# Both token tiles evacuated before their transposes, eleven low parts moved to VectorE, and a fourth bank for small products, in a two-block hybrid layer

## The chip, the cores and the metric

The kernel runs on one core of one Trainium2 chip, as one program of 39576 instructions. The metric is the device time of a run in microseconds; the median of three runs of the kernel before is 2757.88 us. Below, PE is the matrix engine (TensorE), DVE is VectorE, ACT is ScalarE, POOL is GpSimd and SP is the engine that issues most transfers.

## What is computed

The input `x` has 256 tokens of 2048 values. It goes through two blocks, each a mixer and a feed-forward network around residual additions, with shift, scale and gate vectors ("modulation") computed from a conditioning vector:

```
h = rmsnorm(x) * (1 + sc_m) + sh_m ;  x = x + gt_m * rmsnorm(mixer1(h) @ w_out)
h = rmsnorm(x) * (1 + sc_f) + sh_f ;  x = x + gt_f * rmsnorm(relu(h @ w_ff1)**2 @ w_ff2)
u = rmsnorm(x) * (1 + sc1) + sh1   ;  x = x + g1 * (mixer2(u) @ w_out_2)
u = rmsnorm(x) * (1 + sc2) + sh2   ;  x = x + g2 * ((silu(u @ w_gate) * (u @ w_up)) @ w_down)
return rmsnorm(x)
```

`mixer1` holds two linear-attention forms (8 heads each), `mixer2` four attention forms (named fox, nsa, dil and diff in the code). All is float32; the modulation is a vector of 2048 values times a matrix of 2048 x 12288, once for each block.

## The kernel before, in words

**Weights and blocks.** A weight matrix is read in units of 128 x 1024 values (512 KB) into one of five `raw` buffers. ScalarE copies a unit to a rounded high part `wh`; VectorE or GpSimd subtracts it from the unit and writes the low part `wl`; then `raw` is free for the next transfer. High and low parts lie in four or six slots. PE multiplies high by high, high by low and low by high, and adds the three up in PSUM. A `Block` is one slice of output columns (512, or 256 in most of the feed-forward blocks); it takes its units one after the other and its result stays in two of the four PSUM banks named `g`. The units of the modulation are not converted: VectorE multiplies each by a column of the conditioning vector and adds it into `acc` (their transfers and updates stand between those of the weights, in one list, `items`). In the kernel's first part the modulation goes through PE instead, into a PSUM bank of its own (`ps["a"]`, line 2007).

**Small products.** Transposes, attention scores and the like take a bank by `mx()` (line 210) from a ring of three PSUM banks. Who asks for a bank gets that of the third call before, and waits until that product has been read. `run_last` (581) also takes one block's two result banks from this ring (`mbanks`, 503).

**Order of the work.** The order of instructions on each engine is written out by the program itself, with a model of the engines' clocks (`_Clock`). While PE runs a block, `fill` (453) is called after each k-tile (after every second one in blocks of 256 columns, which makes eight calls a block). Each call advances the first generator of the queue `pri` by one step, then one urgent filler, then up to two fillers and up to two weight preparations (`prep`, 285), as the model finds them due. A generator's `yield` ends its step. `run` (567) first empties `pri` down to one generator. Engines work strictly in the order written; an instruction that waits holds back all that stand behind it on its engine.

**The opening blocks.** The first block of each feed-forward network runs on the raw float32 weights, before the others are converted (`run_first`, 607): `("f1",0,0)` with `ev_relu2_s` (1430), `("ga",0,0)` with `ev_gate2_s` (1903). Its results lie with tokens as rows, one bank for each of the two token tiles, and must be transposed. Both functions go through the tiles one after the other: evacuate the tile (ScalarE and VectorE), pause for seven steps, take a bank, four transposes on PE, evacuate again. So the second tile is evacuated after the first one's transposes.

**Where low parts go.** `LOW` (1955 to 1957) gives blocks of the second mixer the value 3; for their units `l_eng` (364) chooses GpSimd or VectorE by the model's clocks, GpSimd unless it would end over 3 us later. Units without a value go to VectorE. `qG` and `kvH` are the first two converted blocks of that mixer, eight units each. `late_prep` (373) reckons with the same choice.

Of the kernel before, what the change touches and what calls it, by code (L numbers as in the profile page):

```python
# [9 lines left out]
F32 = mybir.dt.float32  # L10
# [168 lines left out]
def two_blocks(ctx, tc, I, out):  # L179
    nc = tc.nc  # L180
    PSUM = bass.MemoryType.PSUM
# [12 lines left out]
    def opener(name, side, **kw):  # L194
        cm = tc.tile_pool(name=name, side=side, **kw)
        return cm.__enter__(), partial(cm.__exit__, None, None, None)
# [11 lines left out]
    ps = {}  # L208

    def mx():  # L210
        return ps["m"].tile([128, 512], F32, name="mx", tag="mx")

    def wt(name="wt"):
        return w2.tile([128, 512], F32, name=name, tag="wt")
# [206 lines left out]
    def pri_step():  # L421
        q = pri.popleft()
        try:
            next(q)
        except StopIteration:
            return
        pri.appendleft(q)

    def fill_step(force=False, fillers=fillers):
        k = None  # L430
        for i, (at, q) in enumerate(fillers):
            if force or at <= clk.t["pe"] + lag[0]:
                key = at - lead.get(q, 0.0)
                if k is None or key < best:
                    k, best = i, key
        if k is None:
            return False
        at, q = fillers.pop(k)
        clk.end = 0.0
        try:  # L440
            next(q)
        except StopIteration:
            return True
        fillers.append((clk.end if clk.end else max(at, clk.t["pe"]) + 0.3, q))
        return True
# [3 lines left out]
    def add(q, before=0.0):  # L449
        lead[q] = before  # L450
        fillers.append((clk.t["pe"], q))
# [15 lines left out]
    def drain(until=lambda: False):  # L467
        while (pri or fillers or urgent) and not until():
            if pri:
                pri_step()  # L470
            fill_step(True, urgent)
            fill_step(True)


    def units(w, r0, nkt, c0, n):
        u = []
        for k in range(0, nkt, UK):
            ap = w[r0 + k * 128:r0 + (k + UK) * 128, c0:c0 + n].rearrange("(k p) f -> p k f", p=128)
            u.append(([(0, 128, 0, UK, 0, ap)], UK, n))
        return u  # L480
# [22 lines left out]
    def mbanks():  # L503
        return [mx(), mx()]

    def banks():
        return [psg.tile([128, 512], F32, name="g", tag="g") for _ in range(2)]
# [31 lines left out]
    def run_units(b, pts, idx, pos):  # L539
        for i in idx:  # L540
            prep_to(i + 1)
            it = items[i]
            for kk in range(it["nk"]):
                if b.kind == "S":
                    mm_s(b, pts, it, kk, pos, (0, 1))
                else:
                    mm_t(b, pts, it, kk, pos)
                pos += 1
                if kk == it["nk"] - 1:
                    used(i)  # L550
                if b.n != 256 or kk % 2:
                    fill()
        return pos
# [9 lines left out]
    def add_acc(b, pts, out):  # L563
        for p, a, o in zip(pts, b.acc, out):
            dve.tensor_tensor(o, p, a, op=ADD)

    def run(b):
        while len(pri) > 1:
            clk.end = 0.0
            pri_step()  # L570
            if not clk.end:
                fill_step(True)
        pts = b.pts or banks()
        run_units(b, pts, b.idx, len(b.kts) - sum(items[i]["nk"] for i in b.idx))
        if b.acc:
            add_acc(b, pts, b.acc)
            add(b.done(b.acc))
        elif b.done:
            pri.append(b.done(pts))
# [90 lines left out]
    r = rows[3]  # L670
# [27 lines left out]
    def first_cols():  # L698
        rslots.extend((RAW_BUFS + k, pro) for k in range(3))
        dma_to(len(items))  # L700
        p = mx()
        pe.transpose(p[:, 0:32], rows[3][0:32], ident[0:32, 0:32])
        act.activation(cols[:, 0:32], p[:, 0:32], AF.Copy)
        th = small([32], "th32")
        act.activation(th, p[:, 0:32], AF.Tanh, scale=0.5)
        dve.scalar_tensor_tensor(csil, th, 1.0, cols[:, 0:32], op0=ADD, op1=MUL)
        dve.tensor_scalar(csil, csil, 0.5, None, op0=MUL)

    def more_cols():
        p = mx()  # L710
        for i in range(3):
            pe.transpose(p[:, i * 128:(i + 1) * 128], rows[i], ident)
        act.activation(cols[:, 32:384], p[:, 32:384], AF.Copy)
# [101 lines left out]
    def new_hT(quads=range(4)):  # L815
        if 0 in quads:
            hT["n"] = [0, 0]
        for q in quads:
            t = hT["b", q] = hTp.tile([128, 4, 2, T], FR, name=f"hT{q}", tag=f"hT{q}")
            hT["h", q], hT["l", q] = t[:, :, 0], t[:, :, 1]  # L820
# [90 lines left out]
    def plan(key, b):  # L911
        blocks[key] = b
        order.append(key)
# [496 lines left out]
    def new_r(q):  # L1410
        p = oTp if q < 3 else g["rp"]
        rT[q] = tuple(p.tile([128, 4, T], FR, name=f"r{a}{q}", tag=f"o{a}{q}") for a in "hl")
# [16 lines left out]

    def ev_relu2_s(pts):  # L1430
        new_r(0)
        for t in range(2):
            r = wt("relu")
            act.activation(r, pts[t], AF.Relu)
            dve.scalar_tensor_tensor(r, pts[t], 0.0, r, op0=MAX, op1=MUL)
            for _ in range(7):
                yield
            p = mx()
            for j in range(4):
                pe.transpose(p[:, j * 128:(j + 1) * 128], r[:, j * 128:(j + 1) * 128], ident)  # L1440
            h, l = (x[:, :, t * 128:(t + 1) * 128] for x in rT[0])
            p4 = p.rearrange("p (a b) -> p a b", a=4)
            act.activation(h, p4, AF.Copy)
            dve.tensor_sub(l, p4, h)

    plan(("f1", 0, 0), Block("S", units(w_ff1, 0, KT, 0, 512), list(range(16)), hsrc, ev_relu2_s))
    for ch in range(4):
        for q in range(4):
# [452 lines left out]
        return ev  # L1901

    def ev_gate2_s(pts):
        for t in range(2):
            th = wt("th")
            act.activation(th, pts[t], AF.Tanh, scale=0.5)
            dve.scalar_tensor_tensor(th, th, 1.0, pts[t], op0=ADD, op1=MUL)
            for _ in range(7):
                yield
            p = mx()  # L1910
            for j in range(4):
                pe.transpose(p[:, j * 128:(j + 1) * 128], th[:, j * 128:(j + 1) * 128], ident)
            act.activation(g["sg2"][:, 0, :, t * 128:(t + 1) * 128], p.rearrange("p (a b) -> p a b", a=4), AF.Copy)
            yield

    plan(("ga", 0, 0), Block("S", units(w_g, 0, KT, 0, 512), KS, hsrc, ev_gate2_s))
    for ch, nq in ((0, 4), (1, 4), (2, 3)):
        for q in range(nq):
# [35 lines left out]

    LOW = {k: 1 for k in ("qG", "kvH", "sv", "qA", "kB", "qC", "kD", "dv0", "dv1", "qE", "kF", "fdv")}
    LOW.update({k: 3 for k in LOW if isinstance(k, str)})
    LOW.update({("pA", c): 2 for c in range(4)})
    ai = n_first
    wide = [blocks[n, 0] for n in ("hq", "hf", "hv", "hg", "zq", "zk", "zv", "gg")]
# [49 lines left out]
    x = pro.tile([128, 2, D], F32, name="x")  # L2009
# [155 lines left out]
    g["x"] = xp.tile([128, 2, D], F32, name="xres")  # L2165
    act.dma_start(g["x"], I["x"][0].rearrange("(t p) d -> p t d", p=128))
    drain(lambda: gwn.get("gt_m") == 4)
    run(blocks["oB", 0])
    new_hT(range(3))
    close_more = more_slots("hl2")  # L2170
# [104 lines left out]
    t = hTp.tile([128, 4, 2, T], FR, name="oq2", tag="hT3")  # L2275
# [66 lines left out]
    x = g["x"]  # L2342
# [75 lines left out]
```

## Time and profile before

| what | us |
|---|---|
| median of three runs | 2757.88 |
| lowest and highest run | 2756.11, 2759.71 |
| the profiled execution, its own time | 2756.43 |
| its span, first to last instruction | 2754.7 |
| PE busy in the span | 2629.3 |
| VectorE, ScalarE, GpSimd busy | 1814.2, 1260.8, 410.0 |
| granted clock of PE, mean | 0.981 |

The stages in the span: modulation and first mixer up to about 740 us, first feed-forward network to about 1480, second mixer to about 1990, second feed-forward network to the end. In the timelines a row gives start, length, engine, operation, its output and inputs by name, how many of them, and in brackets how long the engine stood idle before it and what released it. All instructions have line L169, the helper that records them, so they are told apart by names: `mx` is a small product, `g` a block's result, `relu` and `th` what the two functions evacuate, `S` attention scores.

### The profile page before, as it was taken

What the parts mean: (1) busy time and instruction counts of PE and PEld (TensorE: products, weight loads), DVE (VectorE), ACT (ScalarE), POOL (GpSimd) and SP (SyncE); (2) the same over time, 40 slices, a digit from 0 to 9 for tenths busy, and PEclk for the clock granted to TensorE, in tenths of its full rate; (3) what the DMA queues carried; (4) which work ended last, traced back from release to release, by engine and by line L of the source; (5) the groups of instructions that cost most, each with busy time, mean ns of one, the idle gap of its engine ahead of it and who ended that gap; (6) DMA issues with size and microseconds to landing.
All of it is one profiled execution on the core that took longest, in us unless ns stands there. A gap on an engine that the chain in (4) does not pass through costs nothing.

```text
span 2754.7 us, 39576 instructions
## 1 busy us (share of the span) xinstructions
PE 2629.3 (95%) x15073; PEld 2207.5 (80%) x15073; DVE 1814.2 (66%) x2247; ACT 1260.8 (46%) x2124; POOL 410.0 (15%) x262
## 2 busy tenths in 40 slices
PE   7999889899999999999999899898889999999998
PEld 4788879868678888888886888886668888888887
DVE  3557878854667787878854365558756756554566
ACT  2434443444544454444544355544444444443443
POOL 1001242231000000000001555562400000000001
PEclk9999999999999999999999999998999999999999
DMA  9975878985488989989964765666667777666664
GB/s 354 322 255 153 229 201 219 275 253 174 156 267 275 322 286 306 320 279 331 300 191 155 232 186 184 213 225 223 203 207 243 233 247 224 193 194 192 189 187 145
DMA packets 399806, 643.59 MB, mean 234 GB/s; under 512 B 31480, under 2 KB 198088, under 8 KB 398208
## 3 DMA queue, kind: packets, MB, share of 16 engines
q1 hardware_dynamic: 391904, 627.03, 71.7%
q10 hardware_dynamic: 6960, 11.65, 1.2%
q8 instruction: 118, 1.93, 0.3%
q0 software_dynamic: 752, 2.39, 0.2%
q14 instruction: 72, 0.59, 0.1%
HBM read 636.27 MB, written 4.19 MB: 233 GB/s over the span
## 4 chain that ended last, share of the span: by engine, by line
PE 59%; DMA 4%; DVE 4%; POOL 2%; issue 2%; ACT 2%; SPq 0%; POOLq 0%; ACTq 0%; DVEq 0%
PE g L169 56%; PE mx L169 3%; POOL wl L169 1%; DMA raw<-in_w_in_dram 1%; DMA raw<-in_w_out_dram 1%; DVE wl L169 1%; DMA raw<-in_w_ff_dram 1%; ACT wh L169 1%; DVE acc L169 1%; DVE y L169 1%; DVE xres L169 0%; DMA raw<-in_ffn_w_up_dram 0%; DMA raw<-in_ada_w_dram 0%; DMA raw<-in_ffn_w_gate_dram 0%; DVE S L169 0%
## 5 line engine op out<-in xcount | busy, mean ns | idle before, releaser
L169 ACT ACTIVATE wh<-raw 128x1024 fp32r<-128x1024 f32 (+2 forms) x793 | 823.8, 1045 | 896.7 <-PE g L169 406.0
L169 PE MATMUL g<-hT,wh 128*128 128x512 f32 (+1 forms) x4448 | 1218.0, 345 | 9.1 <-ACT wh L169 4.8
L169 DVE TENSOR_TENSOR wl<-raw,wh 128x1024 fp32r<-128x1024 f32 x693 | 858.0, 1245 | 549.8 <-ACT wh L169 545.5
L169 PE MATMUL g<-hT,wl 128*128 128x256 f32 x3376 | 954.9, 283 | 10.3 <-DVE wl L169 5.5
L169 PEld LDWEIGHTS g<-hT,wh 128*128 128x128 f32 x4448 | 772.9, 191 | 125.8 <-issue 18.9
L169 PEld LDWEIGHTS g<-hT,wl 128*128 128x128 f32 x3376 | 644.4, 191 | 14.0 <-DVE wl L169 6.9
L169 DVE SCALAR_TENSOR_TENSOR acc<-raw,csil,acc 128x1024 f32<-128x1024 f32 x276 | 382.3, 1385 | 59.8 <-DMA raw<-in_ada_w_dram 58.6
L169 PE MATMUL g<-wh,rh 128*128 128x512 f32 x864 | 339.0, 392 | 0.0
L169 PE MATMUL g<-wh,rl 128*128 128x512 f32 x864 | 338.9, 392 | 0.0
L169 PE MATMUL g<-wl,rh 128*128 128x512 f32 x864 | 338.6, 392 | 0.0
L169 POOL TENSOR_TENSOR wl<-raw,wh 128x1024 fp32r<-128x1024 f32 (+2 forms) x100 | 230.1, 2311 | 222.7 <-ACT wh L169 211.2
L169 PEld LDWEIGHTS g<-wh,rl 128*128 128x128 f32 x864 | 162.3, 188 | 36.0
L169 PEld LDWEIGHTS g<-wl,rh 128*128 128x128 f32 x864 | 162.4, 188 | 35.7
L169 PEld LDWEIGHTS g<-wh,rh 128*128 128x128 f32 x864 | 162.3, 188 | 35.8
L169 PE MATMUL g<-wh,hT 128*128 128x512 f32 (+2 forms) x544 | 162.9, 371 | 1.8 <-ACT hq L169 1.8
L169 PEld LDWEIGHTS g<-wh,hT 128*128 128x128 f32 x544 | 98.5, 191 | 28.1 <-issue 13.0
L169 POOL TENSOR_TENSOR y<-yy,gw 128x512 f32<-128x512 f32 x6 | 7.7, 1298 | 704.3 <-DVE yy L169 704.3
L169 PE MATMUL g<-wl,hT 128*128 128x512 f32 (+2 forms) x272 | 98.8, 363 | 4.1 <-DVE wl L169 2.0
L169 POOL TENSOR_TENSOR y<-y,gw 128x512 f32<-128x512 f32 x6 | 9.6, 1625 | 558.6 <-DVE y L169 553.2
L169 PE MATMUL g<-raw,y 128*128 128x512 f32 (+1 forms) x192 | 83.9, 580 | 2.8 <-DVE y L169 2.6
L169 PE MATMUL ada<-raw,csil 128*32 128x512 f32 x384 | 67.0, 669 | 7.5 <-DMA raw<-in_w_ada_dram 6.0
L169 PEld LDWEIGHTS g<-raw,y 128*128 128x128 f32 x192 | 34.6, 190 | 36.8 <-issue 30.0
(453 smaller groups left out, 2592.8 us busy)
## 6 DMA issues: line engine op xcount, KB each, us to landing
raw<-in_w_ff_dram SPq DMA_DIRECT2D x256, 512.0 KB, 5.3
raw<-in_w_ada_dram SPq DMA_DIRECT2D x192, 512.0 KB, 5.8
raw<-in_ada_w_dram SPq DMA_DIRECT2D x192, 512.0 KB, 5.2
raw<-in_w_in_dram SPq DMA_DIRECT2D x176, 512.0 KB, 5.9
raw<-in_ffn_w_gate_dram SPq DMA_DIRECT2D x88, 512.0 KB, 4.6
raw<-in_ffn_w_up_dram SPq DMA_DIRECT2D x88, 512.0 KB, 4.7
raw<-in_ffn_w_down_dram SPq DMA_DIRECT2D x88, 512.0 KB, 4.5
raw<-in_w_out_dram SPq DMA_DIRECT2D x60, 512.0 KB, 5.1
```

The source lines that it names most:

```text
L169: r = f(out, *a, **kw)
```

## The change

Three edits. `ev_relu2_s` and `ev_gate2_s` evacuate both token tiles in their first step, keep both, pause for nine and six steps, and then transpose one tile and the other in steps of their own. `qG` and `kvH` are taken out of `LOW`, so all their low parts go to VectorE. After the last modulation product on PE, ahead of the first mixer's last output blocks, the modulation's PSUM bank is closed and opened again as `psx`; from there on every fourth call of `mx()` takes it, so the ring has four banks.

```diff
--- before.py
+++ after.py
@@ -208,6 +208,9 @@
     ps = {}
 
     def mx():
+        ps["k"] = (ps.get("k", 0) + 1) % ps.get("of", 3)
+        if ps["k"] == 3:
+            return ps["x"].tile([128, 512], F32, name="mx", tag="mx4")
         return ps["m"].tile([128, 512], F32, name="mx", tag="mx")
 
     def wt(name="wt"):
@@ -1429,12 +1432,15 @@
 
     def ev_relu2_s(pts):
         new_r(0)
+        rs = []
         for t in range(2):
             r = wt("relu")
             act.activation(r, pts[t], AF.Relu)
             dve.scalar_tensor_tensor(r, pts[t], 0.0, r, op0=MAX, op1=MUL)
-            for _ in range(7):
-                yield
+            rs.append(r)
+        for _ in range(9):
+            yield
+        for t, r in enumerate(rs):
             p = mx()
             for j in range(4):
                 pe.transpose(p[:, j * 128:(j + 1) * 128], r[:, j * 128:(j + 1) * 128], ident)
@@ -1442,6 +1448,7 @@
             p4 = p.rearrange("p (a b) -> p a b", a=4)
             act.activation(h, p4, AF.Copy)
             dve.tensor_sub(l, p4, h)
+            yield
 
     plan(("f1", 0, 0), Block("S", units(w_ff1, 0, KT, 0, 512), list(range(16)), hsrc, ev_relu2_s))
     for ch in range(4):
@@ -1901,12 +1908,15 @@
         return ev
 
     def ev_gate2_s(pts):
+        ths = []
         for t in range(2):
             th = wt("th")
             act.activation(th, pts[t], AF.Tanh, scale=0.5)
             dve.scalar_tensor_tensor(th, th, 1.0, pts[t], op0=ADD, op1=MUL)
-            for _ in range(7):
-                yield
+            ths.append(th)
+        for _ in range(6):
+            yield
+        for t, th in enumerate(ths):
             p = mx()
             for j in range(4):
                 pe.transpose(p[:, j * 128:(j + 1) * 128], th[:, j * 128:(j + 1) * 128], ident)
@@ -1954,6 +1964,8 @@
 
     LOW = {k: 1 for k in ("qG", "kvH", "sv", "qA", "kB", "qC", "kD", "dv0", "dv1", "qE", "kF", "fdv")}
     LOW.update({k: 3 for k in LOW if isinstance(k, str)})
+    for k in ("qG", "kvH"):
+        del LOW[k]
     LOW.update({("pA", c): 2 for c in range(4)})
     ai = n_first
     wide = [blocks[n, 0] for n in ("hq", "hf", "hv", "hg", "zq", "zk", "zv", "gg")]
@@ -2165,6 +2177,9 @@
     g["x"] = xp.tile([128, 2, D], F32, name="xres")
     act.dma_start(g["x"], I["x"][0].rearrange("(t p) d -> p t d", p=128))
     drain(lambda: gwn.get("gt_m") == 4)
+    close_a()
+    ps["x"], close_a = opener("psx", None, bufs=1, space=PSUM)
+    ps["of"] = 4
     run(blocks["oB", 0])
     new_hT(range(3))
     close_more = more_slots("hl2")
```

## Rows read from the trace of the kernel before

**Rows 1.** Page of the kernel before, busy time of each engine.

```profile
PE 2629.3 (95%) x15073; PEld 2207.5 (80%) x15073; DVE 1814.2 (66%) x2247; ACT 1260.8 (46%) x2124; POOL 410.0 (15%) x262
```

**Rows 2.** Waits of PE, whole span: us in total, times, longest.

```profile
PE mx L169 <- DVE S L169: 13.2, 8, 5.3
...
PE mx L169 <- DVE th L169: 8.9, 1, 8.9
...
PE mx L169 <- DVE relu L169: 5.8, 1, 5.8
...
PE mx L169 <- DVE lfp L169: 2.1, 1, 2.1
```

**Rows 3.** Timeline, 770 to 815 us, first opening: start, us, engine, operation [idle before].

```profile
772.62 0.80 PE L169 MATMUL g<-hT,wh 128*128 128x512 f32 x1
...
775.68 0.68 DVE L169 SCALAR_TENSOR_TENSOR relu<-g,relu 128x512 f32<-128x512 f32 x1
...
784.12 0.60 PE L169 MATMUL mx<-c,relu 128*128 128x128 f32 x4
...
786.69 1.23 DVE L169 TENSOR_TENSOR wl<-raw,wh 128x1024 fp32r<-128x1024 f32 x1 [0.25 <-ACT wh L169]
...
786.99 1.06 ACT L169 ACTIVATE wh<-raw 128x1024 fp32r<-128x1024 f32 x1 [0.33 <-DMA raw<-in_w_ff_dram]
...
790.56 1.11 PE L169 MATMUL mx<-c,relu 128*128 128x128 f32 x4 [5.84 <-DVE relu L169]
```

**Rows 4.** Timeline of VectorE, ScalarE and PE, second opening.

```profile
2027.03 0.68 DVE L169 SCALAR_TENSOR_TENSOR th<-th,g 128x512 f32<-128x512 f32 x1
...
2036.52 1.23 DVE L169 TENSOR_TENSOR wl<-raw,wh 128x1024 fp32r<-128x1024 f32 x1 [0.22 <-ACT wh L169]
...
2038.37 1.06 ACT L169 ACTIVATE wh<-raw 128x1024 fp32r<-128x1024 f32 x1 [1.39 <-DMA raw<-in_ffn_w_gate_dram]
...
2041.33 1.11 PE L169 MATMUL mx<-c,th 128*128 128x128 f32 x4 [8.92 <-DVE th L169]
```

**Rows 5.** Four stretches of PE: length, busy, granted clock, DMA share, GB/s.

```profile
790.56:794.25 3.69, 3.69 (x13) 0.50 1.00 340
2041.33:2046.94 5.61, 5.61 (x19) 0.50 0.63 220
1528.12:1534.95 6.83, 6.18 (x29) 0.50 1.08 356
1866.04:1872.87 6.83, 6.42 (x17) 0.50 0.85 298
```

**Rows 6.** Stretches of 10 us in the first feed-forward stage; last: clock, DMA share, GB/s.

```profile
820.00:830.00 10.00, 10.00 (x60) 8.77 (x59) 7.15 (x9) 3.76 (x7) 0.00 (x0) 1.00 0.77 263
...
930.00:940.00 10.00, 10.00 (x45) 8.13 (x44) 7.82 (x8) 4.76 (x5) 0.00 (x0) 1.00 1.04 353
```

**Rows 7.** `wl` on GpSimd, 1500 to 1562; chain of waits; timeline there.

```profile
L169 POOL TENSOR_TENSOR wl<-raw,wh x12: 1397/2392/2867, 1504.0 to 1561.3; 128x1024 fp32r<-128x1024 f32 x11, 128x560 fp32r<-128x560 f32 x1
...
1503.96 2.36 POOL wl L169
...
1518.26 2.36 POOL wl L169
...
1527.87 0.61 PE L169 MATMUL g<-hT,wh 128*128 128x256 f32 x2 [4.31 <-ACT wh L169]
...
1536.69 4.85 DVE L169 TENSOR_TENSOR sq<-sq,sq 128x14 f32<-128x14 f32 x3
```

**Rows 8.** Timeline of PE: small products that wait for a bank.

```profile
1775.28 3.42 PE L169 MATMUL mx<-kD,qC 64*128 64x128 f32 x12 [5.33 <-DVE S L169]
...
1866.45 1.65 PE L169 MATMUL mx<-kF,qE 64*128 64x128 f32 x6 [3.51 <-DVE S L169]
...
1899.34 0.92 PE L169 MATMUL mx<-kF,qE 64*128 64x128 f32 x6 [1.87 <-DVE on L169]
```

**Rows 9.** Waits of all engines, 1490 to 2050 us.

```profile
DVE acc L169 <- DMA raw<-in_ada_w_dram: 60.5, 17, 8.3
```

## The prediction

> **What bounds the kernel now.** I read the page first: the matrix engine (PE) is busy 95% of the span [rows 1], so of the 2754.7 us some 125 are PE idle, and an edit pays only where it takes away one of these idle pieces, or the slow clock that follows a long one. Next I read who PE waited for over the whole span [rows 2]: two waits stand out as single long ones, 8.9 us for `th` and 5.8 us for `relu`; both belong to the two functions of the diff. The timelines around them come next [rows 3, 4], then the granted clock just behind them [rows 5], and the share of time in which the DMA engines are busy in the stage that follows the first [rows 6]. Last the start of the second mixer, where the GpSimd conversions stand [rows 7], and the waits for a bank of the small products [rows 8].
>
> **The two opening blocks.** In rows 3 the first token tile is evacuated early (VectorE at 775.68) and its transposes run at 784.12 at once. The second tile's evacuation is emitted only after seven pauses, that is at the end of the next block. By then ScalarE's in-order queue holds weight conversions, and the last of these could start only at 786.99, when its transfer had landed. The second tile's transposes, put into PE's order right behind the first tile's, wait 5.84 us and start at 790.56. Behind the pause the clock is granted at 0.50, the lower of its two levels (1.2 of 2.4 GHz), until 794.25 [rows 5]: these 3.69 us of PE work would take half at the other level, so 1.85 us more are lost. After the change both evacuations are emitted at the first pause; the second one ends one ScalarE and one VectorE operation later than the first, by 778 at the latest, and the transposes come no earlier than 784. The wait is gone: 5.84 + 1.85 = **7.7 us**.
>
> The same in rows 4: the second tile waits from 2032.4 to 2041.33, 8.92 us, behind a conversion that began only at 2038.37 because of its transfer. From there to 2046.94 the clock stands at 0.50 and PE is busy throughout, 5.61 us [rows 5], of which half is 2.8. After the change the second tanh and its multiply end about 2028.4 (0.7 us behind the first, 2027.03 [rows 4]); with six pauses the transposes fall into the last two steps of the next block, at about 2030 and 2031.5, so the margin is 1.6 us. 8.92 + 2.8 = **11.7 us**.
>
> What is late next? PE now asks for the next block's weights sooner. One block of four weight units runs from 772.62 to 784.12 [rows 3], 2.88 us a unit. With the transposes done at about 785.3, the fourth unit of the next block is wanted at 785.3 + 3 x 2.88 = 793.9; its low part begins at 786.69 and lasts 1.23 us, so it lies ready at 787.9. In the second opening the corresponding units are wanted from 2032.4 on, the fourth by about 2040.7; the conversion at 2036.52 is already for a later block, so all four are there. The transfers behind them: at 820 to 830 us the DMA engines are busy 0.77 of the time, at 930 to 940 all of it [rows 6]. A share of 0.23 of the 50 us from 785 to 835 is 11.5 us of room, more than the 7.7 taken away; so I take the whole, with 0 as the other end for the first opening (the later stage at full DMA takes it back). Behind the second opening the DMA share is 0.63 [rows 5], and nothing takes it back. The splits and the reuse of the product banks move with the transposes and stay off PE's path. No DMA is added or moved by this part.
>
> **Low parts of `qG` and `kvH` on VectorE.** In the stretch that holds both blocks GpSimd makes 12 low parts, 11 of them of 1024 columns at 2392 ns [rows 7]; the eleven go to VectorE at 1.23 us each (the length in rows 3), 13.5 us on an engine that has the time. The chain that ended last goes through three of them (from 1503.96 to 1518.26, 2.36 us each, [rows 7]): each one frees the buffer that the next weight transfer waits for. Per link 2.36 - 1.23 = 1.13 us, in all 3.4 at most. But PE's own long wait here, 4.31 us at 1527.87, is for a conversion that waits for its transfer, so part of this becomes waiting for weights again; between 0 and 3.4 I take half, 1.7. Then a wait of 2.1 us for `lfp` [rows 2]: three VectorE operations of 14 columns take 4.85 us together while GpSimd converts beside them [rows 7]. With GpSimd idle they are short; I take 2.1 of 0 to 2.1. By the Trainium skill (SBUF — State Buffer, Who interferes with whom) a VectorE instruction with two SBUF inputs and a GpSimd one that reads SBUF shut each other out for a whole instruction; the trace agrees (4.85 us for three tiny operations), and by it all of that wait goes. The clock dip of 6.83 us at 1528 [rows 5] costs about 3.1 (half of 6.18 busy); I leave it, as a shorter wait remains, and keep it as the upper end. Together **4 us**, between 8.6 gained and 1.9 lost (a new wait of the length of the smallest in rows 8).
>
> **A fourth bank for small products.** No instruction is added; after the last modulation product every fourth small product gets the freed bank. Its PE waits stand in rows 2 under `S`, 13.2 us in 8 pieces, and three single ones in rows 8. The longest, 5.33 us, is three products waiting for three occupied banks: one bank lets a third of a short burst pass and the rest wait as before; I count 0.5. The 3.51 us wait is the fourth of four products of two heads each, which all fit into four banks: 3.5. The wait of 1.87 us for `on` is of the same kind: 1.9. That is 5.9 us. But this is the stage where PE lives from hand to mouth on weights, so an earlier PE partly waits for them: I take half, **3 us**, with ends of 9 gained (5.9 and the clock dip at 1866, half of 6.42 [rows 5]) and 1.9 lost. By the Trainium skill (Perfetto Trace Analysis, Optimization Strategy) repeated gaps on the engine that should be full can mean that PSUM is too small for the next tile; read as the cause of all eight pieces it would give the whole 13.2 us, and the sum would come to 2721.3. The trace bears that out for two of the three rows only: in the longest the queue of VectorE is late, not the bank.
>
> **Sum.** Against the profiled execution's own 2756.43 us: 2756.43 - 7.7 - 11.7 - 4 - 3 = 2730.0. That execution lies 1.45 us below the median of the runs shown, 2757.88, so the forecast in the measure of the median is **2731.5 us**.
>
> **Rivals.**
> 1. The first feed-forward stage gives its 7.7 us back. For it: DMA engines all busy at 930 to 940. Against: the room at 820 to 830 [rows 6]. 2739.2 us.
> 2. The two mixer edits bring nothing, since transfers set the pace there. For it: the 4.31 us wait is for a transfer [rows 7]. Against: the waits for `lfp`, `S` and `on` are not. 2756.43 - 19.4 + 1.45 = 2738.5 us. Rivals 1 and 2 together: 2746.2.
> 3. The openings do not do what they say: the early evacuation of the second tile is itself stuck behind a conversion that waits for its transfer, and both waits stay. Against: the first tile's evacuation, at whose place it now stands, was on time in both [rows 3, 4]. 2756.43 - 7 + 1.45 = 2750.9 us.
> 4. Slower: VectorE works in order, and its modulation updates wait for their own transfers, 60.5 us in 17 pieces in the second mixer [rows 9], 3.6 us each. Low parts on GpSimd pass them by; on VectorE they queue behind. If seven of the seventeen held a low part back beyond PE's stock of weights, that is 7 x 3.6 = 25.2 us and, with two more clock dips of 3.1, 31.4. The time is then 2756.43 - 19.4 - 3 + 31.4 + 1.45 = 2766.9 us. It decides only where PE has less than 3.6 us of converted weights; at 2.88 us a unit that is little more than one unit. Against: VectorE does the low parts of the feed-forward blocks beside the same updates with PE full.
>
> **Chances.** Forecast 0.55, rival 1 0.19, rival 2 0.14, both 0.04, rival 3 0.03, rival 4 0.05. All unknown terms at their better ends: 2756.43 - 19.4 - 8.6 - 9 + 1.45 = 2720.9; at the worse ends of the mixer's two edits with the openings whole: 2738.5 + 3.8 = 2742.3. The range reaches a little beyond the first for edits that help each other, and to rivals 1 and 2 together: 2719 to 2746. A difference of 0.2%, 5.5 us, is about what a measurement of this kernel can tell from none; all cases but the fourth and a milder form of it lie beyond it on the faster side. Faster 0.91, same 0.05, slower 0.04.
>
> **What would show it.** Right: no PE wait for `relu` or `th` in the list of waits; no dip of the clock at about 787 and 2037; PE busy through the 10 us behind each opening; low parts of `qG` and `kvH` on VectorE and the three tiny `sq` operations short; no 3.5 us wait of `mx<-kF,qE`. Wrong: new PE waits for `wl` or `wh` between 840 and 960 whose sum is near 7 us (rival 1); VectorE idle before a modulation update while PE waits for `wl` at 1500 to 1570 (rival 4); a wait for `relu` or `th` of the old length (rival 3).

## The result and the profile after

The changed kernel takes 2722.76 us in the median (2721.3 to 2726.62) against 2758.8 of the kernel before on the same chip; the ratio is 0.9871, with a 95% interval of 0.9856 to 0.9886, so 36 us less. Measured once more among the experiments, it took 2728.99 us against 2756.46, ratio 0.9897 (0.9882 to 0.9912), 28 us less. The forecast was 2731.5 us, 27 less, within 2719 to 2746. The direction and the range held; the gain is as large as forecast or some us larger.

The page of the changed kernel, busy time of each engine, to be held against [rows 1]:

```profile
PE 2614.4 (96%) x15073; PEld 2198.1 (81%) x15073; DVE 1823.5 (67%) x2259; ACT 1261.0 (46%) x2124; POOL 382.7 (14%) x250
```

Twelve instructions went from GpSimd to VectorE (250 for 262, 2259 for 2247): the eleven low parts of the prediction and one more of 1024 columns in a later block (at 1662 us), which `l_eng` now gives to VectorE. The one of 560 columns in [rows 7] stays on GpSimd. PE is busy 14.9 us less with as many instructions, for the greater part because less of its work ran at the lower clock (granted clock 0.985 in the mean, 0.981 before). Its waits over the whole span (us in total, times, longest), the answer to [rows 2]:

```profile
...
PE g L169 <- POOL wl L169: 8.7, 10, 1.9
...
PE mx L169 <- DVE S L169: 7.4, 4, 5.6
...
PE mx L169 <- ACT ah L169: 4.9, 2, 2.9
```

`relu` and `th` are no longer in the list, and `S` has half of its pieces. The wait of 2.9 us for `ah` is new.

**The first opening.** The timelines of ScalarE, VectorE and PE of the changed kernel, one row or two of each:

```profile
772.10 1.06 ACT L169 ACTIVATE relu<-g 128x512 f32<-128x512 f32 x2
778.58 1.06 ACT L169 ACTIVATE wh<-raw 128x1024 fp32r<-128x1024 f32 x1 [5.42 <-DMA raw<-in_w_ff_dram]
...
773.37 1.28 DVE L169 SCALAR_TENSOR_TENSOR relu<-g,relu 128x512 f32<-128x512 f32 x2
...
782.10 1.04 PE L169 MATMUL mx<-c,relu 128*128 128x128 f32 x8
782.89 0.48 PE L169 MATMUL g<-hT,wh 128*128 128x512 f32 x1
```

Both tiles are evacuated by 774.7, ahead of the conversion that waits 5.42 us for its transfer; all eight transposes run in one piece and the next block follows at once. In [rows 3] four of them waited 5.84 us. The second opening of the changed kernel, in the same views, against [rows 4]:

```profile
2003.62 1.07 ACT L169 ACTIVATE th<-g 128x512 f32<-128x512 f32 x2
...
2004.89 1.28 DVE L169 SCALAR_TENSOR_TENSOR th<-th,g 128x512 f32<-128x512 f32 x2
...
2008.19 0.60 PE L169 MATMUL mx<-c,th 128*128 128x128 f32 x4
...
2010.03 0.60 PE L169 MATMUL mx<-c,th 128*128 128x128 f32 x4
```

The evacuation ends at 2006.2 and the transposes come at 2008.2 and 2010.0, two steps of the block, without a wait. The clock behind both (length, busy, granted clock, DMA share, GB/s; PE alone), against the first two rows of [rows 5]:

```profile
782.10:791.00 8.90, 8.90 (x56) 1.00 0.95 321
866.92:870.33 3.41, 3.32 (x7) 0.50 0.97 348
2008.20:2017.00 8.80, 8.80 (x55) 1.00 0.96 324
```

Full clock behind both openings. The middle row is new: some 85 us later PE waits 2.05 us for `ah`, as it did before (2.19 us), and now the lower level (0.50) is granted behind that wait for 3.41 us. Before it stayed at 1.00 there.

**The second mixer's start.** Low parts, then VectorE's timeline in the changed kernel, against [rows 7]:

```profile
L169 DVE TENSOR_TENSOR wl<-raw,wh x16: 1220/1226/1226, 1494.5 to 1543.7; 128x1024 fp32r<-128x1024 f32 x16
...
1522.63 1.28 DVE L169 SCALAR_TENSOR_TENSOR acc<-raw,csil,acc 128x1024 f32<-128x1024 f32 x1 [1.16 <-DMA raw<-in_ada_w_dram]
1523.84 0.23 DVE L169 RECIPROCAL sq<-sq 128x14 f32<-128x14 f32 x1
1524.11 0.39 DVE L169 TENSOR_TENSOR sq<-sq,sq 128x14 f32<-128x14 f32 x2
1525.58 1.23 DVE L169 TENSOR_TENSOR wl<-raw,wh 128x1024 fp32r<-128x1024 f32 x1 [1.09 <-ACT wh L169]
1526.72 0.17 DVE L169 TENSOR_TENSOR sq<-sq,sq 128x14 f32<-128x14 f32 x1
```

The tiny `sq` products take some 0.2 us each (0.39 for two, 0.17 for one), where three took 4.85. But in VectorE's order a modulation update (1.16 us of waiting for its transfer) and a low part (1.09 us for its high part) stand among them. PE's waits there:

```profile
1514.34 0.50 PE L169 MATMUL g<-hT,wh 128*128 128x256 f32 x2 [2.88 <-ACT wh L169]
1515.60 0.58 PE L169 MATMUL g<-hT,wl 128*128 128x256 f32 x1 [0.76 <-DVE wl L169]
1528.85 0.46 PE L169 MATMUL mx<-c,lfp 128*128 128x128 f32 x2 [1.71 <-DVE lfp L169]
```

The long one is 2.88 for 4.31 us, and `lfp` is still waited for, 1.71 us.

**The fourth bank.** PE's timeline of the changed kernel, at the place of the second of [rows 8]:

```profile
1843.44 1.58 PE L169 MATMUL mx<-kF,qE 64*128 64x128 f32 x16
1854.90 0.49 PE L169 MATMUL mx<-ah,ones_r 128*128 128x512 f32 x1 [2.86 <-ACT ah L169]
```

All 16 run in one piece; the wait of 3.51 us within them is gone. Some 7 us later PE waits 2.86 us for `ah`, a new wait.

### The profile page after: what moved, and what is told of

It is laid out like the page before. It is cut to its first block, busy times and chain, and to the rows that moved or that the text cites. A ratio compares the mean times of both kernels' runs of the same rounds, so it can differ in the third digit from the quotient of the medians.

```text
span 2720.8 us, 39596 instructions
## 1 busy us (share of the span) xinstructions
PE 2614.4 (96%) x15073; PEld 2198.1 (81%) x15073; DVE 1823.5 (67%) x2259; ACT 1261.0 (46%) x2124; POOL 382.7 (14%) x250
## 4 chain that ended last, share of the span: by engine, by line
PE 59%; DVE 4%; DMA 4%; issue 2%; ACT 2%; POOL 1%; SPq 0%; ACTq 0%; POOLq 0%; DVEq 0%
PE g L169 56%; PE mx L169 3%; DMA raw<-in_w_ff_dram 2%; DMA raw<-in_w_in_dram 1%; DVE wl L169 1%; ACT wh L169 1%; DVE acc L169 1%; DMA raw<-in_w_out_dram 1%; POOL wl L169 1%; DMA raw<-in_ada_w_dram 0%; DVE y L169 0%; DVE xres L169 0%; ACT S L169 0%; ACT sq L169 0%; DVE Sc L169 0%
## 5 line engine op out<-in xcount | busy, mean ns | idle before, releaser
L169 DVE TENSOR_TENSOR wl<-raw,wh 128x1024 fp32r<-128x1024 f32 x705 | 871.2, 1243 | 538.4 <-ACT wh L169 536.1
L169 DVE SCALAR_TENSOR_TENSOR acc<-raw,csil,acc 128x1024 f32<-128x1024 f32 x276 | 389.5, 1411 | 58.6 <-DMA raw<-in_ada_w_dram 57.4
L169 POOL TENSOR_TENSOR wl<-raw,wh 128x1024 fp32r<-128x1024 f32 (+2 forms) x88 | 206.0, 2354 | 232.5 <-ACT wh L169 218.8
```

The costliest lines, as they stand in the source:

```text
L169: r = f(out, *a, **kw)
```

## The experiments

Each kernel was timed in five rounds against the kernel before on the same chip; "less" is what the ratio of the two comes to in us. Besides the times I compare lengths of stretches in the traces: from the start of one named instruction to that of another (the first evacuation of `relu` by ScalarE; the first product with `gw` on GpSimd, `y<-yy,gw`; the first evacuations of `kvH`, `qA` and `fdv`; the last of `up`). They are worked out from those starts, and tell what an edit is worth where it stands.

**Each part alone.** The first two kernels are the kernel before with the two opening functions of the diff, or with the first of them only. The other two:

```diff
+    for k in ("qG", "kvH"):
+        del LOW[k]
```

```diff
+        ps["k"] = (ps.get("k", 0) + 1) % ps.get("of", 3)
+        if ps["k"] == 3:
+            return ps["x"].tile([128, 512], F32, name="mx", tag="mx4")
...
+    close_a()
+    ps["x"], close_a = opener("psx", None, bufs=1, space=PSUM)
+    ps["of"] = 4
```

Both openings:

> The kernel before with the two opening blocks alone changed. Theory (the terms of the prediction): the waits for `relu` and `th` and the half clock behind both go and nothing gives them back, 7.7 + 11.7 = 19.4 us less than before; most of the rest of the 36 us by which the changed kernel is faster then belongs to the two mixer edits. Rival A (the first feed-forward stage gives its part back): 11.7 less. Rival B (the openings also bring what the changed kernel gained between the last mixer block and the second opening, where its work stands some 6 us earlier still): 25 or more less, and the two mixer edits together only about 11.

2742.88 us, ratio 0.9941 (0.9925 to 0.9956), 16 less. The first opening alone:

> The kernel before with the first opening block alone changed. Theory: 7.7 us less (the wait of 5.84 for `relu` and 1.85 of half clock), as far as the end. Rival (the first feed-forward stage, where the DMA engines are all busy, gives it back): within 1.5 us of before, with new waits for `wl` or `wh` between 840 and 960 us that sum to about 6.

2750.85 us, ratio 0.9975 (0.9964 to 0.9987), 7 less: the first feed-forward stage does not give it back, and rival A and rival 1 of the prediction fall. The low parts:

> The kernel before with the low parts of `qG` and `kvH` on VectorE, nothing else. Theory: 4 us less by the prediction, 5.5 by the marks of the changed kernel's trace, of which about 2 from `lfp` and from the three tiny `sq` operations and the rest from the chain of weight buffers. Rival A (transfers set the pace here): within 1 us of before. Rival B (VectorE's low parts wait behind the modulation updates, and it only paid because the opening had moved the stage earlier): slower by 2 or more.

2754.13 us, ratio 0.9990 (0.9981 to 0.9998), 2.8 less: not slower, so rival B falls; the interval, 0.6 to 5.2 less, does not tell the theory from rival A, but the stretches below do. The fourth bank:

> The kernel before with the fourth bank for the small products alone. Theory: 3 us less by the prediction; all eight waits for a bank of the second mixer as one rule (a matrix engine that lacks PSUM) would be 9 us, which is also what the marks of the changed kernel's trace leave for it from the end of `kvH` to the second opening (8.2 of shift there). Rival (the waits for a bank turn into waits for weights or for other engines): within 1 us of before, and the wait of 3.5 us before the products of `kF` with `qE` is replaced by one of like length.

2751.07 us, ratio 0.9976 (0.9965 to 0.9987), 6.6 less: over twice the 3 us of the prediction.

**Each part missing.** The parts alone sum to 25.7, the whole had shown 36. So the same three edits were left out of the changed kernel, one at a time.

> The changed kernel with the opening blocks as before: the two mixer edits together. The three parts alone brought 16, 2.8 and 6.6 us, 25.7 in sum, against some 36 for the whole. Theory (the parts only add, and the excess is the uncertainty of four ratios): 9.4 us less than before. Rival (the two mixer edits help each other: the half clock that took 3 us back behind the low parts on VectorE is not there with the fourth bank): 15 to 19 us less.

2747.35 us, ratio 0.9962 (0.9947 to 0.9977), 10.5 less: the theory. PE's waits in it, from 770 to 2060 us:

```profile
...
PE mx L169 <- DVE th L169: 8.7, 1, 8.7
...
PE mx L169 <- DVE relu L169: 6.5, 1, 6.5
```

The two old waits are back.

> The changed kernel with the low parts of `qG` and `kvH` on GpSimd again: openings and fourth bank. Theory (parts add): 16 + 6.6 = 23 us less than before, the wait for `lfp` and the pieces of the chain of `wl` back at the start of the second mixer. Rival (openings and bank help each other): 30 us or more less, so that the low parts are worth 6 at most in the changed kernel.

2732.34 us, ratio 0.9903 (0.9883 to 0.9924), 27 less.

> The changed kernel with three banks for the small products: openings and low parts. Theory (parts add): 16 + 2.8 = 19 us less than before, with the wait of 3.5 us before the products of `kF` with `qE` back and the stretch from `fdv` to the second opening 4 us longer than in the changed kernel. Rival (openings and low parts help each other): 26 us or more less.

2732.56 us, ratio 0.9909 (0.9890 to 0.9927), 25 less. Its PE waits from 1750 to 1900 us, the stage of [rows 8]:

```profile
PE mx L169 <- DVE S L169: 9.8, 2, 5.4
PE mx L169 <- DVE on L169: 1.9, 1, 1.9
```

Without the bank the second wait for `S` (4.4 us of the 9.8) and that for `on` are there again. Both of these last results lie between theory and rival, so the sum was left to a repetition:

> The changed kernel once more, beside the openings alone on the same chip. Added up stretch by stretch from the traces of the runs so far, the parts are worth 6.1 (first opening), 11.8 (second), 5 (low parts) and 6.8 (bank), some 30 us. Theory (the parts add): 30 us less than before, at the lower edge of what the changed kernel showed. Rival (the whole is more than its parts): 36 us again, with the openings alone at 16.

> The two openings alone once more. Theory (the parts add, and the 16 us of the first time were low by chance): 18 us less than before. Rival (the openings alone lose something in the second mixer that the other two edits keep): 16 us or less again.

The whole: 2728.99 us, ratio 0.9897 (0.9882 to 0.9912), 28 less. The openings: 2738.74 us, ratio 0.9937 (0.9924 to 0.9949), 17 less. The first is at the theory, that the parts add, and not at 36; the second, 14 to 21 less by its interval, cannot tell 18 from 16. The stretches say it more sharply, since the noise of the rest of the kernel is not in them (shortest to longest, runs):

```
                             without the edit           with the edit              mean difference
relu to y<-yy,gw             640.6 to 641.8 (4)         633.5 to 637.7 (9)         -5.6  first opening
y<-yy,gw to kvH              151.5 to 156.2 (7)         147.6 to 150.3 (7)         -5.5  low parts
kvH to qA                    50.5 to 52.0 (7)           50.4 to 54.8 (7)           +0.9  low parts
qA to fdv                    244.7 to 247.8 (7)         241.3 to 244.8 (6)         -2.8  bank
fdv to last up, old opening  810.9 to 813.2 (4)         808.5 to 808.8 (2)         -3.8  bank
fdv to last up, 4 banks      808.5 to 808.8 (2)         796.7 to 797.0 (5)         -11.8 second opening
```

Together -28.6, which is 1.0% of the span, between the two measured differences. Three kernels have the new second opening and three banks; their last row is 800.8 to 802.6. By them the second opening is worth 10.9 and the bank 4.7, the same sum. So these two keep their worth, to about 1 us, with the other edit in or out. (The kernel with all low parts on VectorE, below, is left out of `qA` to `fdv`, which it lengthens; the one with late transposes, below, out of the first row.)

**Is it the place of the evacuation or that of the transposes?** The kernel before, with the second tile's evacuation left behind the conversions and its transposes handed to the following block's generator, which emits them four steps after its own evacuation:

```diff
         for t in range(2):
             r = wt("relu")
             act.activation(r, pts[t], AF.Relu)
             dve.scalar_tensor_tensor(r, pts[t], 0.0, r, op0=MAX, op1=MUL)
-            for _ in range(7):
-                yield
...
+            if t == 0:
+                for _ in range(7):
+                    yield
+                turn_r(t, r)
+            else:
+                late_r.append(partial(turn_r, t, r))
```

> The kernel before, with the second tile's evacuation of the first opening left where it was, behind the conversions, and only its four transposes moved half a block later in the order of the matrix engine. Theory (the wait arises because the transposes stand in the matrix engine's order right behind an evacuation that is not ready; either an earlier evacuation or later transposes cures it): no wait for `relu` and no half clock behind it, the same 6 to 7 us less than before as the first opening alone. Rival (only the early evacuation helps: as it is late, its four operations hold the queue of ScalarE and the conversions behind it): a wait for `wh` or `wl` of 3 us or more takes the place of that for `relu` between 784 and 810 us, and the time is within 3 us of before.

2760.93 us, ratio 1.0018 (1.0009 to 1.0028): slower, the stretch from `relu` to `y<-yy,gw` 644.1 us, 2.7 more than without the edit. My theory fell. The timelines of PE, ScalarE and VectorE in that kernel:

```profile
784.94 0.60 PE L169 MATMUL mx<-c,relu 128*128 128x128 f32 x4
785.29 0.48 PE L169 MATMUL g<-hT,wh 128*128 128x512 f32 x1
...
792.22 0.79 PE L169 MATMUL g<-hT,wh 128*128 128x512 f32 x1 [6.34 <-DVE relu L169]
...
788.66 1.06 ACT L169 ACTIVATE wh<-raw 128x1024 fp32r<-128x1024 f32 x1 [0.36 <-DMA raw<-in_w_ff_dram]
...
790.10 1.14 ACT L169 ACTIVATE relu<-g 128x512 f32<-128x512 f32 x3
...
791.49 0.68 DVE L169 SCALAR_TENSOR_TENSOR relu<-g,relu 128x512 f32<-128x512 f32 x1
```

No transpose waits here, and PE waits 6.34 us all the same, for `relu`, in a product of the next block `g`. It is not the weights, as my rival had it, but the product's bank: the opening holds two of the four `g` banks, the next block the other two, and the block after that starts in the banks of the opening. The first half of it (tile 0's bank, free since the first evacuation) starts at 785.29, the other half needs tile 1's bank. ScalarE reads that bank from 790.10 on, behind the row of conversions, and VectorE until 792.17; the product starts at 792.22. So in the kernel before two waits lay one behind the other, and [rows 3] could show only the first. Of the two remedies only the early evacuation takes away both, as the rival's conclusion had it. Early evacuation with the transposes left at their old place was not run. By the Trainium skill (PSUM — Partial Sum Buffer, Engine vs sequencer instructions) matmuls start and complete in program order; the trace agrees, as nothing passes the blocked product in those 6.34 us.

**More low parts on VectorE.** The changed kernel, with `LOW` emptied of all twelve blocks, and with a third block taken out:

```diff
-    for k in ("qG", "kvH"):
+    for k in list(LOW):
         del LOW[k]
```

```diff
-    for k in ("qG", "kvH"):
+    for k in ("qG", "kvH", "sv"):
         del LOW[k]
```

> The changed kernel with the low parts of all twelve blocks of the second mixer's projections on VectorE, not those of the first two alone: a dose of the slower rival's mechanism, VectorE low parts queued behind modulation updates that wait for transfers. Theory (VectorE has the time while it waits for little; GpSimd's 2.4 us links are what is late): within 5 us of the changed kernel either way, since the 8.7 us for which the matrix engine waits on GpSimd low parts go and others on VectorE come. Slower rival: 10 us or more above the changed kernel, the matrix engine waiting for `wl` from VectorE and for `S` and `v` behind them.

2736.9 us, ratio 0.9920 (0.9901 to 0.9939): by the ratios 14 us above the changed kernel's first measurement and 6 above its second, which its interval still touches. The stretch is clearer: `qA` to `fdv` takes 254.0 us, against 243.6 in the mean of the others with four banks. What VectorE waited for in that stretch, in this kernel:

```profile
DVE wl L169 <- ACT wh L169: 48.3, 25, 4.3
...
DVE acc L169 <- DMA raw<-in_ada_w_dram: 0.8, 1, 0.8
```

and in the changed kernel:

```profile
DVE acc L169 <- DMA raw<-in_ada_w_dram: 29.1, 11, 6.7
...
DVE wl L169 <- ACT wh L169: 11.7, 6, 3.3
```

So the slower rival of the prediction is real at this dose, but with another wait in it: what stands in VectorE's order and waits is the low part itself, for ScalarE's high part (48.3 us for 11.7), not the modulation update for its transfer (0.8 for 29.1). Of the 10.1 us by which this stretch is longer than in the changed kernel, 3.3 are PE idle and 6.8 PE busy, with the clock granted at 0.95 for 0.98. PE's longest wait is 6.9 us for scores (`ACT S`), at a place where the changed kernel waits 5.6 too; for VectorE's `wl` it waits only 1.2 us in all. That the waiting low parts hold up what PE then waits for is argued here, not shown.

> The changed kernel with the low parts of a third block, `sv`, on VectorE too. Theory: the matrix engine waits 1.4 us for GpSimd's low parts between 1460 and 1600 us in the changed kernel; these go, and nothing else does: within 2.5 us of the changed kernel. Slower rival (VectorE falls behind from here on, as it did with all twelve blocks, where 14 us were lost): 3 us or more above the changed kernel.

2729.5 us, ratio 0.9904 (0.9891 to 0.9917), the same as the changed kernel beside it (2728.99). No version here beats the changed kernel.

This kernel's profile also shows one thing that makes executions differ. From the evacuation of `kvH` to that of `qA` (length, PE busy, granted clock, DMA share, GB/s) it has

```profile
1556.70:1611.20 54.50, 52.73 (x462) 0.91 0.75 231
```

and the changed kernel

```profile
1554.50:1605.60 51.10, 49.72 (x461) 0.97 0.81 247
```

PE has the same instructions to do, is idle 1.8 and 1.4 us, and of 3.4 us of difference 3 are PE time at the lower clock. The kernel with the low parts alone has 54.8 us and 0.91 there. The repetition of the changed kernel, the same program, has 50.4 us and 1.00, for 51.1 and 0.97. Such dips, in a place or not, are the reason why small parts are better measured by stretches.

## Why the prediction was right

**The openings, 19.4 forecast.** Second opening: 11.7 forecast, 11.8 found (10.9 beside three banks), wait and half clock. First: 7.7 forecast, 5.6 found in the mean. The two runs with the new opening in which the clock did not fall at all in the stretch are 633.5 and 634.1 us long, 7.6 below the mean of the old one: the whole of the term. In the seven others a dip of 3.41 us (twice 6.83) stands behind the wait for `ah`, as in the row at 866.92, and half of it is lost, 1.7 us. So little came back as waiting for weights (rival 1; at most 0.6 us, for `wl`, in two kernels): the room that the prediction read in [rows 6] was there. What came back did so through the clock behind the wait for `ah`, which the prediction had not reckoned with, and in the three kernels with new openings alone also in that wait itself (2.95 to 3.79 us for 2.19). Of the wait's cause the prediction named one half, the transposes in PE's order. The other, the product bank, it passed over with "the reuse of the product banks move with the transposes and stay off PE's path". The bank moves with the evacuation, not with the transposes, and under a late evacuation it lies on PE's path. The number came out right because the edit moves the evacuation too and so takes away both; that is luck as far as the bank goes. (The list of waits before holds two more single ones as long, 9.1 us for a constant at the start and 6.0 for `hgA` in the first mixer; the prediction passed over them, and no edit touches them.)

**Low parts, 4 forecast.** 5.5 found where they stand, 4.6 with the dips behind. Its inner working was off in both terms, in opposite directions. `lfp`: 2.1 forecast, 0.4 found (1.71 left of 2.1). The prediction took the wait for a matter of three slow operations; these are short now, and as VectorE stands still for a transfer and for a high part in between, the time is still spent. What the prediction worked out from the Trainium skill (SBUF — State Buffer, Who interferes with whom), that the whole wait goes, did not come; the trace agrees with the page on the cause of the 4.85 us, and shows that it was not the only thing that `lfp` waited for. The weights: 1.7 of at most 3.4 was forecast, half of it to be lost to transfers. Found: the two waits for GpSimd's low parts before the long one, 1.17 and 1.09 us, are gone and the long one is 1.43 shorter (4.31 to 2.88), 3.7 us together, all of the upper end. That makes 4.1 of the 5.5; the rest is PE's clock. Behind the long wait the lower level lasts 3.41 us in the changed kernel, for 6.83 [rows 5], a part that the prediction kept for its upper end (length, busy, granted clock, DMA share, GB/s):

```profile
1515.45:1518.86 3.41, 3.26 (x15) 0.50 1.24 287
```

In three of the other kernels with this edit the lower level still lasts 6.83 us there. The halving was the mistake: transfer, high part and low part are in series there, and 1.13 us less on one link is 1.13 us less on the chain. The chain of waits of the changed kernel shows the pattern, three rows of it:

```profile
1495.73 3.70 DMA raw<-in_w_in_dram
1499.45 1.07 ACT wh L169
1500.55 1.24 DVE wl L169
```

**The fourth bank, 3 forecast.** This is the term that was mis-sized: 6.6 found (2.8 + 3.8). The prediction halved the waits that it expected to go, since others would come. That is what happened, as the waits of PE in the kernel with the bank alone show, from the last evacuation of `dv` to that of the second of the blocks that read `o2h`:

```profile
PE mx L169 <- DVE S L169: 5.8, 2, 5.3
...
PE g L169 <- ACT wh L169: 2.3, 1, 2.3
PE mx L169 <- ACT ah L169: 2.2, 1, 2.2
PE mx L169 <- DVE v L169: 1.4, 1, 1.4
```

The longest piece for `S` stays (5.3), the 3.51 us are gone, `ah` (2.2) is new, and in place of 1.87 for `on` stand 1.4 for `v` and the small piece of `S`. The same stretch as a whole (length, PE busy, granted clock, DMA share, GB/s), in the kernel before and in that with the bank alone:

```profile
1767.90:1925.40 157.50, 139.00 (x785) 0.91 0.67 217
```

```profile
1770.50:1921.00 150.50, 133.42 (x784) 0.93 0.70 228
```

It is 7.0 us shorter, and only 1.4 of that is idle time (157.50 - 139.00 = 18.5 before, 17.1 now). The other 5.6 us are PE's busy time. Some 3.2 of them are the clock: the dip of 6.83 us at 1866, with 6.42 us of busy time [rows 5], is gone. Another 1.7 are products that now run side by side. The 36 products of `S` with `dv`, 128*64 in size, come in groups of four; in the kernel before each group runs by itself, with the fourth bank two groups run together at two places (granted clock 1.00 in both rows; the kernel before, then that with the bank alone):

```profile
1814.30 0.86 PE L169 MATMUL mx<-S,dv 128*64 128x256 f32 x4
...
1815.29 0.88 PE L169 MATMUL mx<-S,dv 128*64 128x256 f32 x8
```

Eight products take 0.88 us there, four 0.86; in all, the 36 keep PE busy for 6.1 us, for 7.8 before. The last 0.7 us of busy time stays open. The prediction had that dip in its upper end alone, half of 6.42, and expected at the middle nothing from the clock. That step failed, and the second gain, from the products side by side, it did not see; in the two openings the same reckoning, wait plus half of the dip behind it, had been made and was right. As to the reading of "too little PSUM" behind all 13.2 us of waits for `S` (the Trainium skill, Perfetto Trace Analysis, Optimization Strategy): in the changed kernel 7.4 us of them remain, 5.6 in one piece that the queue of VectorE sets, so the trace bears the rule out for a part of the pieces, as forecast. What makes VectorE late in that piece, the longest wait of the stage, is what made `lfp` late: two operations of 4 columns take 2.3 us each while GpSimd converts (1752.04 to 1760.01), and 0.15 us in the kernel with all low parts on VectorE, where GpSimd does not. The changed kernel, then that one:

```profile
1755.43 2.31 DVE L169 TENSOR_TENSOR colt<-red,cols 128x4 f32<-128x4 f32 x1
1757.77 2.26 DVE L169 SCALAR_TENSOR_TENSOR Affn<-colt,cols 128x4 f32<-128x4 f32 x1
...
1761.17 0.15 DVE L169 TENSOR_TENSOR colt<-red,cols 128x4 f32<-128x4 f32 x1
```

**The sum.** 26.4 forecast, 28.6 found by stretches, 28 and 36 by the two measurements. The terms were off by -2.1, +0.1, +0.6 and +3.6 us; the first makes up for part of the last, so that the sum came out as near as it did is in part luck. Rivals 1 and 2 gave 2739.2 and 2738.5; neither shows beyond the small waits named above. Rival 3 fails by the timelines of the two openings above. Rival 4's mechanism shows in small (the 1.16 and 1.09 us before `lfp`) and costs time only when all twelve blocks are moved, with the other wait in it. What I leave open: why the first measurement of the changed kernel stands some 7 us beyond the sum of its parts and the second at it. The executions of the second themselves lie from 2720.59 to 2729.86; dips of the clock are shown as one source of such differences, not as the only one.

## What to carry to other kernels

When PE waits for an evacuation, ask what else the late evacuation holds: here moving the waiting transposes away only uncovered a wait of 6.34 us for the PSUM bank that the same tile still occupied, so evacuate at once and transpose later, not the other way. Price a wait of PE together with the stretch at the lower clock behind it; in the stage of the fourth bank that part (3.2 us) was over twice the idle time (1.4). And a gain on a chain of transfer, high part and low part in series is not to be halved before it is seen that the next link waits for something else.

## What the runs showed of the hardware

The granted clock does not follow the length of a single wait alone. Behind the wait for `ah` in the first feed-forward stage, of 2.05 us in the changed kernel and 1.94 in its repetition, it fell to 0.50 for 3.41 us. Behind waits at the same place of 2.19 us in the kernel before, 2.18 in the kernel without the changed openings and 2.18 in the one without the bank it stayed at 1.00. In the kernel with late transposes it fell even behind 1.32 us:

```profile
880.73:884.14 3.41, 3.41 (x10) 0.50 0.98 350
```

Half of it, 1.7 us, is most of the 2.7 us that this kernel lost in the stretch. Of the 14 kernels traced, the five that waited longer there (2.27 to 3.79 us) all had a dip. So a wait that cost nothing beyond itself can begin to cost a dip when the work ahead of it changes by a few us, and the same wait may carry one in one kernel and none in the next.
